# Five norms of a one-layer encoder step: two exact matmuls against a constant matrix and Newton's steps on VectorE, in place of sums by rows, a power on GpSimd and a spread by the identity

## The chip, the core and the metric

The kernel runs on one core of one Trainium2 chip. The metric is device time in microseconds (us) for one launch; less is better. The core's engines are named here as in the profile: TensorE (PE, with its weight loads as PEld), VectorE (DVE), ScalarE (ACT), GpSimd (POOL) and SyncE (SP, which issues most DMAs).

## The reference, cut to what matters

One layer over 320 rows (256 of a prompt, 64 of a running stream), model width 2048, in fp32:

```python
def rmsnorm(x, g):
    y = xf * lax.rsqrt(jnp.mean(xf * xf, axis=-1, keepdims=True) + EPS)
    return y * g
z = rmsnorm(x, ln_g) @ w_in                       # 2048 x 3328: q, k, v, gMLP u and v
q, k = rmsnorm(q, q_g), rmsnorm(k, k_g)           # per head of 64
a_o = sink_attention(...)                         # banded, T5 bias, sinks
s_o = u * (W_s rmsnorm(v) + b)                    # after GELU
mix = concat([rmsnorm(a_o, g_a), rmsnorm(s_o, g_s)])
x = x + mix @ w_out                               # 2048 x 2048
h = rmsnorm(x, ln_ffn)
return x + square(relu(h @ w_up)) @ w_down        # 2048 x 8192, 8192 x 2048
```

The outputs are the new x and the new k, v and normalised v rows.

## The kernel before, in words

Activations are kept transposed: a tile has 128 channels on the partitions and the T = 320 rows of the sequence along the free axis. A norm over channels is therefore a sum over partitions, and its result, one number for each of the 320 rows of the sequence, is needed on every partition.

Every matrix product runs in exact parts: weights and activations are split into a high part (fp32r, a Copy on ScalarE, `w_hi`) and a low part (the difference, on VectorE, `w_lo`), and three matmuls of 128x320 are summed (high x high, low activations x high weights, high activations x low weights), L106 to L138. A weight chunk is 4 tiles of the inner dimension by 256 columns, that is 24 matmuls. `w_hi` and `w_lo` have 3 buffers each, so that the split of a chunk starts when the chunk three places ahead has been used up.

A product of 256 output columns ("a group") is summed in one of two PSUM tiles named `acc` (`ps_acc`, 2 buffers). So group n+2 can't start on TensorE before the result of group n was read out of PSUM. For the product with `w_out` (L464 to L475) a group has 48 matmuls for each half of the inner dimension (half 0: attention, `AH`/`AL`; half 1: gMLP, `SH`/`SL`), and it is read out by

```python
469  nc.vector.tensor_tensor(out=t, in0=ps[:, :, 0:T], in1=rm[:, None, :].to_broadcast([P, 2, T]), op=ALU.mult)
```

The factor `rm`, the inverse root of the mean square of `a_o` or `s_o`, is applied here, after the product, so that the product itself needn't wait for it. The read-out must: it is the first place that needs `rm`. In the same way `rx` (norm of x) is needed by the read-outs of the first product (L257, L258, L267), `rk` (norm of k) by L289, and `r2` by L488.

An inverse root is computed in two functions before. `rstd_rows` (L154) sums squares over partitions by three fp32 matmuls with the data as weights and a column of 1/n as the moving side, so that a row of the sequence lands on a partition; VectorE adds eps, GpSimd takes the power -0.5. `spread` (L165) multiplies these 128x3 numbers, broadcast, with the identity in three fp32 matmuls and copies the 128x320 result out of PSUM. The norm of k does the same for two heads (L261, L283 to L289). An fp32 matmul runs as two passes in the trace. The norm of the gMLP's v (`rv`, L414) uses `rstd_rows` alone.

The order of instructions on each engine is fixed when the program is built: the tile framework schedules by its own timeline, and each engine then works through its list in order. A late instruction thus holds up all that stands behind it in its engine's list.

Of the kernel before, what the change touches and what calls it, by code (L numbers as in the profile page):

```python
# [29 lines left out]
def hymba_step_kernel(ctx: ExitStack, tc: tile.TileContext, i, o):  # L30
    nc = tc.nc

    const = ctx.enter_context(tc.tile_pool(name="const", bufs=1))
    actp = ctx.enter_context(tc.tile_pool(name="actp", bufs=2))
    wp = ctx.enter_context(tc.tile_pool(name="wp", bufs=3))
    sm = ctx.enter_context(tc.tile_pool(name="sm", bufs=2))
    phase1 = ExitStack()
    at = phase1.enter_context(tc.tile_pool(name="at", bufs=2))
# [20 lines left out]
    g_q, g_k = cols[:, 48:49], cols[:, 49:50]  # L59
# [15 lines left out]
    warm_ps = misc()  # L75
    for _ in range(3):
        nc.tensor.matmul(out=warm_ps[:, 0:256], lhsT=idle[:, 0:128], rhs=idle[:, 0:256], start=True, stop=True)
    inv_dm = const.tile([P, 1], F32, name="inv_dm")
    nc.vector.memset(inv_dm, 1.0 / DM)
    inv_1k = const.tile([P, 1], F32, name="inv_1k")  # L80
    nc.vector.memset(inv_1k, 1.0 / 1024)
    hone = const.tile([P, 2], F32, name="hone")
    nc.vector.memset(hone, 0.0)
    nc.vector.memset(hone[0:HD, 0:1], 1.0)
    nc.vector.memset(hone[HD:P, 1:2], 1.0)
    hsel = const.tile([P, 2], F32, name="hsel")
    nc.vector.memset(hsel, 0.0)
    nc.vector.memset(hsel[0:HD, 0:1], 1.0 / HD)
    nc.vector.memset(hsel[HD:P, 1:2], 1.0 / HD)
# [16 lines left out]
    def products(w, k0, nk, jobs, rh, rl, first=None, deep=None):  # L106
# [4 lines left out]
        for a, n in chunks(nk, first is not None):  # L111
# [4 lines left out]
            for j, (c0, ps) in enumerate(jobs):  # L116
# [21 lines left out]
                steps.append((high.ins, low.ins, mm.ins))  # L138

    def sums(name):  # L140

        t = sm.tile([P, TP], F32, name=name, tag="ssq", bufs=2)
        nc.gpsimd.memset(t[:, T:TP], 0.0)
        return t

    def acc_tile():
        return ps_acc.tile([P, 2, 512], F32, name="acc", tag="acc")
# [3 lines left out]
        products(w, k0, nk, [(c0, ps)], rh, rl, deep=deep)  # L151
        return ps

    def rstd_rows(sq, weight, eps, h=1):  # L154

        st = misc()
        for t in range(3):
            nc.tensor.matmul(out=st[:, t * h:t * h + h], lhsT=sq[:, t * P:(t + 1) * P], rhs=weight, start=True, stop=True)  # L158
        r = sm.tile([P, 3 * h], F32, name="r_rows", tag="r_rows")
        nc.vector.tensor_scalar(out=r, in0=st[:, 0:3 * h], scalar1=eps, scalar2=None, op0=ALU.add)  # L160
        rs = sm.tile([P, 3 * h], F32, name="rs_rows", tag="rs_rows")
        nc.gpsimd.tensor_tensor(out=rs, in0=r, in1=nhalf[:, 0:3 * h], op=ALU.pow)
        return rs

    def spread(rs, name):  # L165

        bc = misc()
        for t, (t0, n) in enumerate(TT):
            nc.tensor.matmul(out=bc[:, t0:t0 + n], lhsT=rs[:, t:t + 1].to_broadcast([P, P]),  # L169
                             rhs=ident[:, 0:n], start=True, stop=True)  # L170
        out = sm.tile([P, T], F32, name=name, tag="rstd_b", bufs=2)
        nc.vector.tensor_copy(out=out, in_=bc[:, 0:T])
        return out
# [21 lines left out]
    q0_ps = ps_sc.tile([P, 2, 512], F32, name="q0_ps", tag="s_ps")  # L195
    products(w_in, 0, KT, [(1024, kv_ps), (0, q0_ps)], xh, xl, first=load_x)

    kvx = blk("kvx", [P, 1152])
    kn = kvx[:, 0:448]
    vT = kvx[:, 448:768]  # L200
    rkx = kvx[:, 768:1152].rearrange("p (t c) -> p t c", t=3)
    nc.sync.dma_start(out=kn[:, 256:384], in_=i["ckT"])


# [38 lines left out]
    ssq2 = sm.tile([P, 2, T], F32, name="ssq2", tag="w2", bufs=4)  # L243
    for k in range(0, KT, 2):
        sq = sm.tile([P, 2, T], F32, name="sq2", tag="w2", bufs=4) if k else ssq2
# [2 lines left out]
        if k:  # L248
            nc.vector.tensor_tensor(out=ssq2, in0=ssq2, in1=sq, op=ALU.add)
    ssq = sums("ssq")  # L250
    nc.vector.tensor_tensor(out=ssq[:, 0:T], in0=ssq2[:, 0], in1=ssq2[:, 1], op=ALU.add)

    rx = spread(rstd_rows(ssq, inv_dm, EPS), "rx")


    zk = sm.tile([P, T], F32, name="zk", tag="w2", bufs=4)
    nc.vector.tensor_tensor(out=zk, in0=kv_ps[:, 0, 0:T], in1=rx, op=ALU.mult)  # L257
    nc.vector.tensor_tensor(out=vT, in0=kv_ps[:, 1, 0:T], in1=rx, op=ALU.mult)  # L258
    sq = sums("ksq")
    nc.scalar.activation(out=sq[:, 0:T], in_=zk, func=AF.Square)  # L260
    rk = rstd_rows(sq, hsel, EPS, 2)  # L261

    rq = at.tile([P, 4, 10], F32, name="rq", bufs=1)

    def queries(g, q_ps):
# [8 lines left out]
        for b in range(5):  # L274
# [8 lines left out]
    nc.scalar.activation(out=rkx.rearrange("p t (h d) -> p (t h) d", h=2), in_=rk[:, :, None].to_broadcast([P, 6, HD]),  # L283
                         func=AF.Copy)
    bc = misc()
    for t, (t0, n) in enumerate(TT):
        nc.tensor.matmul(out=bc[:, t0:t0 + n], lhsT=rkx[:, t], rhs=ident[:, 0:n], start=True, stop=True)
    for dst, c in ((kn[:, 0:256], slice(0, 256)), (kn[:, 384:448], slice(256, 320))):
        nc.vector.scalar_tensor_tensor(out=dst, in0=zk[:, c], scalar=g_k, in1=bc[:, c], op0=ALU.mult, op1=ALU.mult)  # L289
    for h in range(2):  # L290
        hs = slice(h * HD, (h + 1) * HD)
        nc.vector.tensor_scalar(out=kz[hs, h, h], in0=kn[hs], scalar1=g_q[hs], scalar2=None, op0=ALU.mult)
# [110 lines left out]
        nc.vector.scalar_tensor_tensor(out=out, in0=c, scalar=1.0, in1=z, op0=ALU.add, op1=ALU.mult)  # L403

    gv = blk("gv", [P, 8, T])
    acc_v = sums("acc_v")
    for g in range(4):
        attend_next((4, 3, 3, 0)[g])
        v_ps = product(w_in, 0, KT, 2304 + g * 256, xh, xl)
# [8 lines left out]
    for t, (t0, n) in enumerate(TT):  # L418
        for h in range(2):
# [3 lines left out]
            dst = vnat[:, t] if t < 2 else vnat_s[0:HD]  # L423
            nc.scalar.activation(out=dst[:, h * 512:(h + 1) * 512], in_=vps[0:n], func=AF.Copy, scale=rv[0:n, t:t + 1])
    nc.gpsimd.dma_start(out=o["sgu_v"], in_=vnat_s[0:HD])
    for g in range(8):
        sp_ps = misc()
        cs = slice(g * P, (g + 1) * P)
        for b in range(2):
# [3 lines left out]
                                in0=sp_ps[:, 0:256].rearrange("p (b i) -> p b i", b=2),  # L433
                                in1=sgb[:, g, None, :].to_broadcast([P, 2, P]), op=ALU.add)
# [136 lines left out]
```

## Time and profile before

| what | value |
|---|---|
| median of 3 runs | 1263.6 us (1261.91 to 1265.82) |
| profiled execution, its own time | 1262.26 us |
| its span | 1259.7 us |
| TensorE busy | 1252.3 us, 99% |
| VectorE busy | 637.9 us, 51% |
| ScalarE busy | 489.4 us, 39% |
| GpSimd busy | 106.1 us, 8% |

The profile is of one execution. A row of its timeline says when an instruction started, how long it took, its engine, its line in the kernel, what it wrote and read, and in square brackets for how long the engine had been idle and what released it. The chain is the sequence of work that ended last, followed back from the end. The profiled execution lies 1.3 us under the median of the runs.

### The profile page before, as it was taken

To read this page: it belongs to the slowest core of one execution; us is meant where nothing else is said; L and a number is where in the kernel's file an instruction comes from. 1 tells how busy PE (TensorE), PEld (TensorE's weight loads), DVE (VectorE), ACT (ScalarE), POOL (GpSimd) and SP (SyncE) were. 2 spreads that over 40 slices of the span, in tenths; PEclk is the share of its full clock that TensorE was granted. 3 is DMA by queue.
4 is the path that set the end of the run, shared out by engine and by line. 5 is a ranking of instruction groups with operands and counts; after the bars stand their busy time and mean duration, and the time that the engine had idled before them with its cause. 6 is when DMAs were issued, how large, how long until landed. Compare 5 with 4: busy or idle time off the path is not lost.

```text
span 1259.7 us, 20182 instructions
## 1 busy us (share of the span) xinstructions
PE 1252.3 (99%) x8519; PEld 1236.6 (98%) x8519; DVE 637.9 (51%) x731; ACT 489.4 (39%) x636; POOL 106.1 (8%) x104
## 2 busy tenths in 40 slices
PE   8999999999999999999999999999999999999998
PEld 7998889999999999999999999999999999999998
DVE  7547857756864444444444444444444334444443
ACT  7335546533543342223333333343333333343221
POOL 2213452400310000000000000000000000000000
PEclk9999999999999999999999999999999999999999
DMA  8643233644454444445544444455444444444550
GB/s 281 191 136 116 85 109 119 216 148 137 151 149 148 152 149 149 149 147 150 150 150 151 150 151 151 151 151 151 150 151 150 146 148 149 148 153 160 169 169 32
DMA packets 186426, 187.77 MB, mean 149 GB/s; under 512 B 6464, under 2 KB 185856, under 8 KB 186336
## 3 DMA queue, kind: packets, MB, share of 16 engines
q1 hardware_dynamic: 185696, 185.43, 47.2%
q8 instruction: 66, 1.08, 0.4%
q0 software_dynamic: 496, 1.03, 0.3%
q14 instruction: 24, 0.20, 0.0%
q10 hardware_dynamic: 144, 0.03, 0.0%
HBM read 182.91 MB, written 3.32 MB: 148 GB/s over the span
## 4 chain that ended last, share of the span: by engine, by line
PE 98%; DMA 0%; SPq 0%; ACT 0%; issue 0%; DVE 0%
PE acc L136 93%; PE misc L136 1%; PE q_ps L136 1%; PE s_ps L329 1%; PE misc L374 1%; PE misc L365 1%; DMA xT<-in_xT 0%; SPq L99 0%; PE misc L275 0%; PE misc L430 0%; PE misc L158 0%; PE misc L422 0%; PE misc L169 0%; ACT XH L178 0%; PE misc L431 0%; ACT w_hi L125 0%
## 5 line engine op out<-in xcount | busy, mean ns | idle before, releaser
L126 DVE TENSOR_TENSOR w_lo<-w_raw,w_hi 128x1024 fp32r<-128x1024 f32 x332 | 413.6, 1246 | 460.6 <-ACT w_hi L125 451.2
L125 ACT ACTIVATE w_hi<-w_raw 128x1024 fp32r<-128x1024 f32 x332 | 351.9, 1060 | 708.0 <-PE acc L136 674.6
L136 PE MATMUL acc<-H2H,w_hi 128*128 128x320 f32 x1024 | 316.6, 309 | 0.0
L136 PE MATMUL acc<-H2L,w_hi 128*128 128x320 f32 x1024 | 316.4, 309 | 0.0
L136 PE MATMUL acc<-H2H,w_lo 128*128 128x320 f32 x1024 | 316.4, 309 | 0.0
L136 PE MATMUL acc<-FH,w_hi 128*128 128x320 f32 x992 | 306.5, 309 | 0.0
L136 PE MATMUL acc<-FL,w_hi 128*128 128x320 f32 x992 | 306.5, 309 | 0.0
L136 PE MATMUL acc<-FH,w_lo 128*128 128x320 f32 x992 | 306.5, 309 | 0.0
L136 PEld LDWEIGHTS acc<-H2L,w_hi 128*128 128x128 f32 x1024 | 192.2, 188 | 0.0
L136 PEld LDWEIGHTS acc<-H2H,w_hi 128*128 128x128 f32 x1024 | 192.2, 188 | 0.0
L136 PEld LDWEIGHTS acc<-H2H,w_lo 128*128 128x128 f32 x1024 | 192.2, 188 | 0.0
L136 PEld LDWEIGHTS acc<-FH,w_hi 128*128 128x128 f32 x992 | 186.2, 188 | 0.0
L136 PEld LDWEIGHTS acc<-FL,w_hi 128*128 128x128 f32 x992 | 186.2, 188 | 0.0
L136 PEld LDWEIGHTS acc<-FH,w_lo 128*128 128x128 f32 x992 | 186.2, 188 | 0.0
L136 PE MATMUL acc<-XH,w_hi 128*128 128x320 f32 x384 | 117.2, 316 | 1.2 <-ACT w_hi L125 1.1
L136 PE MATMUL acc<-XH,w_lo 128*128 128x320 f32 x384 | 116.8, 315 | 0.0
L136 PE MATMUL acc<-XL,w_hi 128*128 128x320 f32 x384 | 116.6, 314 | 0.0
L136 PEld LDWEIGHTS acc<-XH,w_hi 128*128 128x128 f32 x384 | 71.2, 189 | 4.7 <-ACT w_hi L125 2.2
L136 PEld LDWEIGHTS acc<-XL,w_hi 128*128 128x128 f32 x384 | 71.4, 189 | 2.4 <-issue 1.9
L136 PEld LDWEIGHTS acc<-XH,w_lo 128*128 128x128 f32 x384 | 71.1, 188 | 2.2 <-issue 1.5
L488 DVE SCALAR_TENSOR_TENSOR tf<-acc,r 128x640 f32<-128x640 f32 x32 | 26.4, 825 | 42.7 <-PE acc L136 42.7
L502 DVE TENSOR_TENSOR xT<-xT,acc 128x640 f32<-128x640 f32 x31 | 25.5, 821 | 41.8 <-PE acc L136 41.8
(176 smaller groups left out, 1016.9 us busy)
## 6 DMA issues: line engine op xcount, KB each, us to landing
w_raw<-in_w_up SPq DMA_DIRECT2D x128, 512.0 KB
w_raw<-in_w_down SPq DMA_DIRECT2D x128, 512.0 KB
w_raw<-in_w_in SPq DMA_DIRECT2D x44, 512.0 KB
w_raw<-in_w_out SPq DMA_DIRECT2D x32, 512.0 KB
w_first<-in_w_in SPq DMA_DIRECT2D x6, 512.0 KB
out_yT<-xT SPq DMA_DIRECT2D x7, 320.0 KB
xT<-in_xT SPq DMA_DIRECT2D x3, 640.0 KB
w_first<-in_w_in SPq DMA_DIRECT2D x8, 128.0 KB
```

What stands on the lines that cost most here:

```text
L125: high = pin(nc.scalar.activation(out=hi[:, :n], in_=raw[:, :n], func=AF.Copy))
L126: low = pin(nc.vector.tensor_tensor(out=lo[:, :n], in0=raw[:, :n], in1=hi[:, :n].bitcast(F32), op=ALU.subtract))
L136: mm = nc.tensor.matmul(out=out, lhsT=w_[:, k, g * P:(g + 1) * P], rhs=r_(kk), start=(kk == 0 and x == 0), stop=(kk == nk - 1 and x == 2))
L329: nc.tensor.matmul(out=s_ps[:, j, 0:2 * nk].rearrange("x (p k) -> x p k", p=2), lhsT=qT[:, blk_, a:a + 2].rearrange("p a t -> p (a t)"), r ...
L365: nc.tensor.transpose(out=pt_ps[0:n, (2 * p + j) * P:(2 * p + j + 1) * P], in_=s[:, p, j, c:c + n], identity=ident)
L374: nc.tensor.matmul(out=o_ps[p * HD:(p + 1) * HD, 0:256], lhsT=v[0:n, kv], rhs=pt[0:n, p * 256:(p + 1) * 256], start=(x == 0), stop=(x == l ...
L488: nc.vector.scalar_tensor_tensor(out=t, in0=ps[:, :, 0:T], scalar=0.0, in1=r2[:, None, :].to_broadcast([P, 2, T]), op0=ALU.max, op1=ALU.mult)
L502: nc.vector.tensor_tensor(out=xT[:, a:a + n], in0=xT[:, a:a + n], in1=p, op=ALU.add)
```

## The change

Five norms (`rx`, `rk`, `rm0`, `rm1`, `r2`) get a new function `rstd`. The squares, already summed over the tiles of channels, are split into a high part (ScalarE) and a low part (VectorE); two fp32r matmuls of 128x320 with a constant 128x128 matrix as weights (1/2048, 1/1024, or two blocks of 1/64 for the heads of k) give the mean on all partitions at once. Then VectorE works on 128x320 numbers: eps is added, a first guess of the inverse root is made from the integer bits, and three Newton steps of three instructions each follow, that is eleven instructions after the split. The sums lose their padding to 384 columns (only that of v keeps it), and GpSimd writes three constant matrices at the start. `rv` and the norm of q stay as they were.

```diff
@@ constants
-    inv_dm = const.tile([P, 1], F32, name="inv_dm")
-    nc.vector.memset(inv_dm, 1.0 / DM)
+    mean_dm = const.tile([P, P], F32R, name="mean_dm")
+    nc.gpsimd.memset(mean_dm.bitcast(F32), 1.0 / DM)
+    mean_1k = const.tile([P, P], F32R, name="mean_1k")
+    nc.gpsimd.memset(mean_1k.bitcast(F32), 1.0 / 1024)
...
@@ the norm
-        nc.gpsimd.tensor_tensor(out=rs, in0=r, in1=nhalf[:, 0:3 * h], op=ALU.pow)
-    def spread(rs, name):
-        bc = misc()
-        for t, (t0, n) in enumerate(TT):
-            nc.tensor.matmul(out=bc[:, t0:t0 + n], lhsT=rs[:, t:t + 1].to_broadcast([P, P]),
-                             rhs=ident[:, 0:n], start=True, stop=True)
-        out = sm.tile([P, T], F32, name=name, tag="rstd_b", bufs=2)
-        nc.vector.tensor_copy(out=out, in_=bc[:, 0:T])
+    def rstd(acc, mean, eps, out):
+        hl = sm.tile([P, 2, T], F32R, name="n_hl", tag="w2", bufs=4)
+        hi, lo = hl[:, 0], hl[:, 1]
+        nc.scalar.activation(out=hi, in_=acc, func=AF.Copy)
+        nc.vector.tensor_tensor(out=lo, in0=acc, in1=hi.bitcast(F32), op=ALU.subtract)
+        ps = misc()
+        nc.tensor.matmul(out=ps[:, 0:T], lhsT=mean, rhs=hi, start=True, stop=False)
+        nc.tensor.matmul(out=ps[:, 0:T], lhsT=mean, rhs=lo, start=False, stop=True)
+        xt = sm.tile([P, 2, T], F32, name="n_xt", tag="w2", bufs=4)
+        x, t = xt[:, 0], xt[:, 1]
+        nc.vector.tensor_scalar(out=x, in0=ps[:, 0:T], scalar1=eps, scalar2=3e38, op0=ALU.add, op1=ALU.min)
+        nc.vector.tensor_scalar(out=out.bitcast(I32), in0=x.bitcast(I32), scalar1=-0.5, scalar2=float(0x5F3759DF),
+                                op0=ALU.mult, op1=ALU.add)
+        for _ in range(3):
+            nc.vector.tensor_tensor(out=t, in0=out, in1=out, op=ALU.mult)
+            nc.vector.scalar_tensor_tensor(out=t, in0=t, scalar=-0.5, in1=x, op0=ALU.mult, op1=ALU.mult)
+            nc.vector.scalar_tensor_tensor(out=out, in0=t, scalar=1.5, in1=out, op0=ALU.add, op1=ALU.mult)
         return out
...
@@ the five places
-    rx = spread(rstd_rows(ssq, inv_dm, EPS), "rx")
+    rx = rstd(ssq, mean_dm, EPS, rstd_b("rx"))
...
-    rk = rstd_rows(sq, hsel, EPS, 2)
+    rk = rstd(sq, mean_hd, EPS, rstd_b("rk"))
...
-        rm = spread(rstd_rows(acc, inv_1k, EPS), f"rm{half}")
+        rm = rstd(acc, mean_1k, EPS, rstd_b(f"rm{half}"))
...
-    r2 = spread(rstd_rows(acc_x, inv_dm, EPS), "r2")
+    r2 = rstd(acc_x, mean_dm, EPS, rstd_b("r2"))
```

The schedule is built anew, and so the lists of the engines change beyond the five places. On VectorE, at the first norm of the product with `w_out` (`rm` of half 0), the list was, from the split of one weight chunk to that of the next but one (`to` is the read-out of a group, `SL` a low part of the gMLP's output, `xT` the residual add):

```order
L126 TENSOR_TENSOR w_lo<-w_raw,w_hi 128x1024
L172 COPY rm_2640<-misc 128x320
L179 SCALAR_TENSOR_TENSOR SL<-gv,cols,SH 128x320 x2
L469 TENSOR_TENSOR to<-acc,rm_2640 128x640
L471 TENSOR_TENSOR xT<-xT,to 128x640
L126 TENSOR_TENSOR w_lo<-w_raw,w_hi 128x1024
L469 TENSOR_TENSOR to<-acc,rm_2640 128x640
```

One copy stood between the matmul that spread the root and the read-out, and the read-outs of the first and the second group stood one chunk apart.

The same place of VectorE's list now, behind the two `SL` and the first two instructions of the norm (eps, first guess); lines are those of the changed file, `n_xt` holds x and t of the Newton steps:

```order
L182 TENSOR_TENSOR n_xt<-rm_2636 128x320
L130 TENSOR_TENSOR w_lo<-w_raw,w_hi 128x1024
L183 SCALAR_TENSOR_TENSOR n_xt<-n_xt 128x320
L184 SCALAR_TENSOR_TENSOR rm_2636<-n_xt,rm_2636 128x320
L182 TENSOR_TENSOR n_xt<-rm_2636 128x320
L183 SCALAR_TENSOR_TENSOR n_xt<-n_xt 128x320
L130 TENSOR_TENSOR w_lo<-w_raw,w_hi 128x1024
L184 SCALAR_TENSOR_TENSOR rm_2636<-n_xt,rm_2636 128x320
L182 TENSOR_TENSOR n_xt<-rm_2636 128x320
L183 SCALAR_TENSOR_TENSOR n_xt<-n_xt 128x320
L184 SCALAR_TENSOR_TENSOR rm_2636<-n_xt,rm_2636 128x320
L479 TENSOR_TENSOR to<-acc,rm_2636 128x640 x2
```

The read-out of the first group now stands behind all eleven instructions and behind two more weight splits, which are those of the sixth and the seventh chunk of this half; the read-outs of the first two groups stand side by side.

The second norm of this product (half 1) on VectorE now, behind eps, first guess and two instructions of the first step:

```order
L130 TENSOR_TENSOR w_lo<-w_raw,w_hi 128x1024
L184 SCALAR_TENSOR_TENSOR rm_3167<-n_xt,rm_3167 128x320
L182 TENSOR_TENSOR n_xt<-rm_3167 128x320
L183 SCALAR_TENSOR_TENSOR n_xt<-n_xt 128x320
L184 SCALAR_TENSOR_TENSOR rm_3167<-n_xt,rm_3167 128x320
L130 TENSOR_TENSOR w_lo<-w_raw,w_hi 128x1024
L182 TENSOR_TENSOR n_xt<-rm_3167 128x320
L183 SCALAR_TENSOR_TENSOR n_xt<-n_xt 128x320
L184 SCALAR_TENSOR_TENSOR rm_3167<-n_xt,rm_3167 128x320
L479 TENSOR_TENSOR to<-acc,rm_3167 128x640 x2
```

Here the two splits between are those of the fifth and the sixth chunk of the half. Before, one copy (L172) and nothing else stood between a weight split and the read-out.

On TensorE the two matmuls with the constant matrix stand between main matmuls: in half 0 behind 61 and behind 68 of them (the first two groups have 96), in half 1 behind 29 and behind 43, at `rx` behind 6 and behind 9 of the 96 of its group.

## Rows read from the trace of the kernel before

**Rows 1.** The page: busy time of the engines, and the chain by engine.
```profile
PE 1252.3 (99%) x8519; PEld 1236.6 (98%) x8519; DVE 637.9 (51%) x731; ACT 489.4 (39%) x636; POOL 106.1 (8%) x104
...
PE 98%; DMA 0%; SPq 0%; ACT 0%; issue 0%; DVE 0%
```

**Rows 2.** Timeline of TensorE at `r2`: start us, us, engine, line, operation.
```profile
361.69 0.72 PE L158 MATMUL misc<-inv_dm,acc_x 128*128 128x1 f32 x6
...
362.51 0.31 PE L136 MATMUL acc<-H2L,w_hi 128*128 128x320 f32 x1
...
367.20 0.78 PE L169 MATMUL misc<-ident,rs_rows 128*128 128x128 f32 x6
...
368.02 0.31 PE L136 MATMUL acc<-H2L,w_hi 128*128 128x320 f32 x1
```

**Rows 3.** The chain from 367 us on: start us, us, what.
```profile
367.98 874.34 PE acc L136 x5961
```

**Rows 4.** Timeline of TensorE: first matmul of half 0, last of its second group.
```profile
238.45 0.31 PE L136 MATMUL acc<-AH,w_hi 128*128 128x320 f32 x1
...
253.72 0.31 PE L136 MATMUL acc<-AH,w_lo 128*128 128x320 f32 x1
```

**Rows 5.** Timeline of VectorE at the norm of half 0.
```profile
247.35 1.23 DVE L126 TENSOR_TENSOR w_lo<-w_raw,w_hi 128x1024 fp32r<-128x1024 f32 x1 [0.74 <-ACT w_hi L125]
248.50 0.48 DVE L172 COPY rm<-misc 128x320 f32<-128x320 f32 x1
248.90 1.86 DVE L179 SCALAR_TENSOR_TENSOR SL<-gv,cols,SH 128x320 fp32r<-128x320 f32 x2
250.68 0.81 DVE L469 TENSOR_TENSOR to<-acc,rm 128x640 f32<-128x640 f32 x1
251.52 0.82 DVE L471 TENSOR_TENSOR xT<-xT,to 128x640 f32<-128x640 f32 x1
```

**Rows 6.** Timelines of ScalarE and GpSimd in the same stretch.
```profile
248.40 0.55 ACT L178 ACTIVATE SH<-gv,cols 128x320 fp32r<-128x320 f32 x1
250.45 1.06 ACT L125 ACTIVATE w_hi<-w_raw 128x1024 fp32r<-128x1024 f32 x1 [1.50 <-issue]
253.97 1.06 ACT L125 ACTIVATE w_hi<-w_raw 128x1024 fp32r<-128x1024 f32 x1 [2.46 <-PE acc L136]
...
247.76 2.65 POOL L386 TENSOR_TENSOR acc_s<-acc_s,sq 128x320 f32<-128x320 f32 x2 [4.01 <-ACT sq L385]
```

**Rows 7.** Timeline of VectorE: a product out of PSUM, and a tensor_scalar.
```profile
45.05 0.49 DVE L257 TENSOR_TENSOR zk<-acc,rx 128x320 f32<-128x320 f32 x1
...
240.74 0.52 DVE L400 TENSOR_SCALAR gc<-gc 128x640 f32<-128x640 f32 x1
```

**Rows 8.** Timeline of VectorE at the norm of half 1.
```profile
302.59 0.48 DVE L172 COPY rm<-misc 128x320 f32<-128x320 f32 x1
304.69 0.82 DVE L469 TENSOR_TENSOR to<-acc,rm 128x640 f32<-128x640 f32 x1 [1.62 <-PE acc L136]
```

**Rows 9.** Timeline of TensorE: first matmul of the group behind `rx`.
```profile
37.76 0.31 PE L136 MATMUL acc<-XH,w_hi 128*128 128x320 f32 x1
```

**Rows 10.** Timeline of TensorE in the first 14 us.
```profile
1.29 2.93 PE L77 MATMUL misc<-idle 128*128 128x256 f32 x6 [1.29 <-DVE hsel L87]
4.27 0.90 PE L136 MATMUL acc<-XH,w_hi 128*128 128x320 f32 x2
4.97 0.74 PE L136 MATMUL acc<-XL,w_hi 128*128 128x320 f32 x2
...
6.82 0.46 PE L136 MATMUL acc<-XH,w_lo 128*128 128x320 f32 x2
7.12 0.46 PE L136 MATMUL q_ps<-XH,w_lo 128*128 128x320 f32 x2
...
13.51 0.56 PE L136 MATMUL q_ps<-XH,w_hi 128*128 128x320 f32 x2 [1.53 <-ACT w_hi L125]
```

**Rows 11.** Stretches: PE, PEld, DVE, ACT, POOL busy, PEclk, DMA share, GB/s.
```profile
4.00:6.00 2.00, 1.89 (x6) 1.27 (x6) 1.08 (x3) 0.90 (x3) 1.82 (x4) 1.00 0.94 285
```

More of the change, by code (lines that the diff above doesn't have):

```diff
@@ L10 @@
 F32R = mybir.dt.float32r
+I32 = mybir.dt.int32
 AF = mybir.ActivationFunctionType
@@ L77, in hymba_step_kernel @@
         nc.tensor.matmul(out=warm_ps[:, 0:256], lhsT=idle[:, 0:128], rhs=idle[:, 0:256], start=True, stop=True)
-    inv_dm = const.tile([P, 1], F32, name="inv_dm")
-    nc.vector.memset(inv_dm, 1.0 / DM)
     inv_1k = const.tile([P, 1], F32, name="inv_1k")
     nc.vector.memset(inv_1k, 1.0 / 1024)
+    mean_dm = const.tile([P, P], F32R, name="mean_dm")
+    nc.gpsimd.memset(mean_dm.bitcast(F32), 1.0 / DM)
+    mean_1k = const.tile([P, P], F32R, name="mean_1k")
+    nc.gpsimd.memset(mean_1k.bitcast(F32), 1.0 / 1024)
+    mean_hd = const.tile([P, P], F32R, name="mean_hd")
+    nc.gpsimd.memset(mean_hd.bitcast(F32), 0.0)
+    for h in range(2):
+        nc.gpsimd.memset(mean_hd[h * HD:(h + 1) * HD, h * HD:(h + 1) * HD].bitcast(F32), 1.0 / HD)
     hone = const.tile([P, 2], F32, name="hone")
@@ L85, in hymba_step_kernel @@
     nc.vector.memset(hone[HD:P, 1:2], 1.0)
[L86 to L89, printed above, removed]
     loads, between, steps = [], [], []
@@ L140, in sums @@
     def sums(name):
-        t = sm.tile([P, TP], F32, name=name, tag="ssq", bufs=2)
-        nc.gpsimd.memset(t[:, T:TP], 0.0)
-        return t
+        return sm.tile([P, T], F32, name=name, tag="ssq", bufs=2)
     def acc_tile():
@@ L152, in product, with rstd_rows @@
         return ps
-    def rstd_rows(sq, weight, eps, h=1):
+    def rstd_rows(sq, weight, eps):
         st = misc()
         for t in range(3):
[L158 to L161, printed above, removed]
-        nc.gpsimd.tensor_tensor(out=rs, in0=r, in1=nhalf[:, 0:3 * h], op=ALU.pow)
-        return rs
@@ L165, in spread @@
-    def spread(rs, name):
-        bc = misc()
-        for t, (t0, n) in enumerate(TT):
-            nc.tensor.matmul(out=bc[:, t0:t0 + n], lhsT=rs[:, t:t + 1].to_broadcast([P, P]),
-                             rhs=ident[:, 0:n], start=True, stop=True)
-        out = sm.tile([P, T], F32, name=name, tag="rstd_b", bufs=2)
-        nc.vector.tensor_copy(out=out, in_=bc[:, 0:T])
-        return out
+            nc.tensor.matmul(out=st[:, t:t + 1], lhsT=sq[:, t * P:(t + 1) * P], rhs=weight, start=True, stop=True)
@@ new lines, in rstd_rows @@
+        r = sm.tile([P, 3], F32, name="r_rows", tag="r_rows")
+        nc.vector.tensor_scalar(out=r, in0=st[:, 0:3], scalar1=eps, scalar2=None, op0=ALU.add)
+        rs = sm.tile([P, 3], F32, name="rs_rows", tag="rs_rows")
+        nc.gpsimd.tensor_tensor(out=rs, in0=r, in1=nhalf[:, 0:3], op=ALU.pow)
+        return rs
+    def rstd(acc, mean, eps, out):
[15 more added lines that the diff above has]
+            nc.vector.scalar_tensor_tensor(out=out, in0=t, scalar=1.5, in1=out, op0=ALU.add, op1=ALU.mult)
+        return out
@@ L175, in split, with rstd_b @@
+    def rstd_b(name):
+        return sm.tile([P, T], F32, name=name, tag="rstd_b", bufs=2)
     def split(src, g, hi, lo, pinned=False):
@@ L196, in hymba_step_kernel @@
     products(w_in, 0, KT, [(1024, kv_ps), (0, q0_ps)], xh, xl, first=load_x)
-    kvx = blk("kvx", [P, 1152])
+    kvx = blk("kvx", [P, 768])
     kn = kvx[:, 0:448]
     vT = kvx[:, 448:768]
-    rkx = kvx[:, 768:1152].rearrange("p (t c) -> p t c", t=3)
     nc.sync.dma_start(out=kn[:, 256:384], in_=i["ckT"])
@@ L250, in hymba_step_kernel @@
     ssq = sums("ssq")
-    nc.vector.tensor_tensor(out=ssq[:, 0:T], in0=ssq2[:, 0], in1=ssq2[:, 1], op=ALU.add)
-    rx = spread(rstd_rows(ssq, inv_dm, EPS), "rx")
+    nc.vector.tensor_tensor(out=ssq, in0=ssq2[:, 0], in1=ssq2[:, 1], op=ALU.add)
+    rx = rstd(ssq, mean_dm, EPS, rstd_b("rx"))
     zk = sm.tile([P, T], F32, name="zk", tag="w2", bufs=4)
@@ L259, in hymba_step_kernel @@
     sq = sums("ksq")
-    nc.scalar.activation(out=sq[:, 0:T], in_=zk, func=AF.Square)
-    rk = rstd_rows(sq, hsel, EPS, 2)
+    nc.scalar.activation(out=sq, in_=zk, func=AF.Square)
+    rk = rstd(sq, mean_hd, EPS, rstd_b("rk"))
     rq = at.tile([P, 4, 10], F32, name="rq", bufs=1)
@@ L281, in hymba_step_kernel @@
     queries(0, q0_ps)
[L283 to L287, printed above, removed]
     for dst, c in ((kn[:, 0:256], slice(0, 256)), (kn[:, 384:448], slice(256, 320))):
-        nc.vector.scalar_tensor_tensor(out=dst, in0=zk[:, c], scalar=g_k, in1=bc[:, c], op0=ALU.mult, op1=ALU.mult)
+        nc.vector.scalar_tensor_tensor(out=dst, in0=zk[:, c], scalar=g_k, in1=rk[:, c], op0=ALU.mult, op1=ALU.mult)
     for h in range(2):
@@ L405, in hymba_step_kernel @@
     gv = blk("gv", [P, 8, T])
-    acc_v = sums("acc_v")
+    acc_v = at.tile([P, TP], F32, name="acc_v", bufs=1)
+    nc.gpsimd.memset(acc_v[:, T:TP], 0.0)
     for g in range(4):
```

## The prediction

> **What bounds the kernel now.** I read the page's busy times first, then the chain, then the timelines of the engines at each of the five norms. The page shows TensorE busy for 99% of the span, and the chain that ended last is TensorE's work for 98% of it [rows 1]. From 367 us to the end the chain is one unbroken piece of 5961 main matmuls in 874.34 us, 0.1467 us each [rows 3]. The view of waits shows no wait of TensorE from 36 us on that is worth naming. Two things follow. A pass taken off TensorE shortens the run by that pass. And a wait put on TensorE lengthens it by the whole wait, because nothing behind it has slack to give back. The other engines have time to spare on average (VectorE 51%), but each works its list in order, so what counts is when the one instruction that TensorE waits for comes up.
>
> **Passes removed.** At `r2` the six passes that sum by rows start at 361.69, and the second main matmul behind them at 362.51: 0.82 us for six passes and one main matmul, so 0.82 - 0.147 = 0.67 us. The six that spread the root run from 367.20 to 368.02, the same 0.67 [rows 2]. So 1.35 us a norm; the norm of k has the same six and six passes, with two columns in place of one, and I take the same. Five norms: 6.73 us.
>
> **Matmuls added.** Two fp32r matmuls of 128x320 a norm. They are of the main matmuls' shape and kind, so 2 x 0.1467 = 0.29 [rows 3], 1.47 us for five. Net on TensorE: -5.27 us.
>
> **VectorE's chain.** Each norm now has eleven instructions in a row, each needing the one before. A product of 128x320 out of PSUM takes 0.49 us [rows 7], and a dependent instruction starts 0.03 behind the end of the one before (250.68 + 0.81, then 251.52) [rows 5]: 0.52 a step. The first guess is a tensor_scalar out of SBUF; one of 128x640 took 0.52 [rows 7], so half of that with some fixed part, 0.35. Nothing in the trace does integer bits; bounds are 0.25 and 0.52. Together 0.53 + 0.35 + 9 x 0.52 = 5.6 us, without the weight splits that stand between (1.15 us each, from 247.35 to the next start at 248.50 [rows 5]). Before, it was one copy of 0.48. Who waits for it differs at each place.
>
> **`rm` of half 0: a wait of about 5.6 us.** I count on the clock of before from the first matmul of the half, at 238.45 [rows 4]. The second mean matmul stands behind 68 main ones and the first mean: 238.45 + 68 x 0.1467 + 0.15 = 248.57, done 0.31 later at 248.9. VectorE's list has the two `SL` ahead of the norm. The second `SH` that they need ended at 248.95, and beside GpSimd's sums (247.76 to 250.4 [rows 6]) the pair took 1.86 [rows 5]; a little earlier than before, as the copy ahead is gone, they end near 249.8 (bounds 249.4 and 250.6). Then eps, guess and one product: 251.2. Then the split of the sixth chunk, 252.35. Then four steps, 2.1 us: 254.4. Then the split of the seventh chunk. Its `w_hi` can't start before the fourth chunk is used up, which is the last of the second group: 238.45 + 96 x 0.1467 + 0.29 = 252.83. In before `w_hi` started at 253.97, 0.1 behind that point (253.72 is the last matmul, 253.87 its successor [rows 4, 6]), and took 1.06; so it is there at 254.0 and the split runs to 255.55. Four more steps: 257.65. Read-out 0.82: 258.45. TensorE, with the third group next, needs the bank at 252.83. Wait: 5.6 us. Before, the read-out ended at 251.5 [rows 5] against a need at 253.87, a reserve of 2.4 us. The lower bound is firm if steps take what I say: the seventh chunk's split cannot start before 254.05, whatever VectorE did earlier, and 254.05 + 1.15 + 2.1 + 0.82 = 258.1, a wait of 5.3. The upper, with the late end of `SL` and steps of 0.6: 6.8.
>
> **`rm` of half 1: about 1.3 us.** From the first matmul of the half as zero: second mean done at 44 x 0.1467 + 0.31 = 6.8. Eps, guess, two products: 8.7. The fifth chunk's `w_hi` is there at 7.33 + 0.1 + 1.06 = 8.5, so its split ends at 9.85; four steps, 11.95; the sixth chunk's `w_hi` is there at 10.86 + 1.16 = 12.0, split to 13.2; three steps, 14.8; read-out 15.6. TensorE needs the bank at 96 x 0.1467 + 0.29 = 14.4. Wait 1.3, bounds 0.6 and 2.3. Before, the read-out started when the group ended, with `rm` there 1.6 us earlier [rows 8].
>
> **The other three: nothing.** At `rx` the second mean is done at 37.76 + 9 x 0.1467 + 0.15 + 0.31 = 39.5 [rows 9]; eleven steps and two or three splits end near 48.3, and the read-outs of k and v near 49.3. Their bank is needed when the next group but one starts, 96 matmuls behind 37.76, at 52.1: a reserve of 2.8. The next weight split then ends near 51.2 for a need at 52.4, a reserve of 1.2, the smallest of the hidden ones. `rk` feeds k for the attention, which starts some 20 us later. At `r2` a group has 96 matmuls, so 14 us more lie between the mean and the need, and the chain with splits takes some 10. The power on GpSimd, the padding memsets and VectorE's copies go from places where TensorE didn't wait. GpSimd's new constants are written in the first microseconds, while TensorE runs out of data anyway (1.53 us before 13.51 [rows 10]); if that cover were gone, it would be under 1 us. No DMA is added or moved past another; the loads on SP keep their order.
>
> **The clock.** The first main matmuls ran 0.35 us apart (4.27 to 4.97 is two), those at 6.82 and 7.12 0.15 apart [rows 10]: the lower level, 1.2 GHz, and then the upper, 2.4, though the stretch row gives a granted clock of 1.00 there too [rows 11], so I go by the spacing. The lower level held from the first matmul at 1.29 to about 6.5, 5.2 us. After a pause of 1.53 us the level was still the upper one. A pause of 5.6 us does not occur in this trace. If the clock falls in it, I price it by the start: 5.2 us at half pace lose 2.6 us. Bounds 0 and 3.5.
> The Trainium skill, "TensorE: Matmul & The Clock Gate", section "HAM oscillation", says that a long enough wait of TensorE puts the clock back to half and that the matmuls behind the wait start slow. By that rule the clock falls here; the trace's shorter pauses neither show nor exclude it.
>
> **Sum.** -5.27 + 5.6 + 1.3 = +1.6 without the clock, +4.2 with it. Against the profiled execution's 1262.26 us (span 1259.7) that is 1263.9 and 1266.5. The runs' median is 1.3 us higher; on its scale 1265.2 and 1267.8.
>
> **Rivals.**
> (a) *Both waits and the clock falls*: 1267.8. Chance 0.45; my forecast.
> (b) *Both waits, clock stays up*: 1265.2, within 0.3%, not slower. The place is the third group of half 0; it decides whether a pause of 5.6 us is long enough, and all I have is that 1.53 is not. Chance 0.29.
> (c) *No wait at half 0*: TensorE only loses passes, and the time is 1263.6 - 5.3 + 1.3 = 1259.6, or 1258.3 if half 1 doesn't wait either. For that the root must be ready at 252.0, 3.1 us behind the mean, where eleven instructions need 5.6 by the nearest rows; against it speaks also the seventh chunk's split, which alone comes later. It would take VectorE steps at a third of the price, or a third group that doesn't need this read-out. Chance 0.11.
> (d) *The steps are dearer and a third wait appears*: at 0.70 a step, `rx` ends 1.7 us later, which uses up the reserve of 1.2 by 0.5, half 0 waits 0.7 more, half 1 some 1.0 more: 1270. Chance 0.15. The new order of the attention and gMLP stages, whose lists changed too, falls under this.
>
> **How the numbers follow.** A measurement of this kernel can tell about 0.3%, 3.8 us. (a) lies just above that with an own range of 1265.5 to 1269.5, and about 0.65 of it is slower by more than 0.3%; of (b) hardly any, of (d) most: slower 0.29 + 0.02 + 0.14 = 0.45. Faster by over 0.3% is the part of (c) with no wait at all, and something for a stage that I misread: 0.10. The rest, 0.45, within 0.3%. The range of 1260 to 1271 leaves out the better half of (c) and the far end of (d).
>
> **What would show it.** In the profile after: TensorE idle once for 5 to 6 us before the third group of half 0, near 251 us on its clock (the passes saved by then make it some 2 us earlier), released by VectorE's L479; once for about 1.3 us near 308; no wait at the other norms. Main matmuls 0.29 us apart for some microseconds behind the first wait would show (a), 0.147 at once (b). The work of five norms on TensorE falls from 60 passes to 10. Wrong would be: no wait at half 0 (then the steps are cheap), or a wait at `rx`.

## The result and the profile after

The changed kernel took 1269.65 us (median of 4 runs, 1269.37 to 1270.42) against 1264.26 for the kernel before, measured beside it (1261.91 to 1265.82): a ratio of 1.0043, 95% interval 1.0031 to 1.0055. It is slower, by 5.4 us; predicted were +4.2 and 1267.8 us. The profiled execution of after took 1270.42 us, with a span of 1268.6. Executions of one kernel differ by up to some 3 us at the start. Counted from a fixed mark behind the start (the matmul with the one-hot table, which stands at the same place of the program in every run; below it is called the mark), after's trace is 6.0 us longer than either trace of before; the table under "before_again" has this for every run.

The page of after, busy times and the chain, as in [rows 1]:

```profile
PE 1253.2 (99%) x8469; PEld 1237.1 (98%) x8469; DVE 661.2 (52%) x778; ACT 490.4 (39%) x640; POOL 100.8 (8%) x99
...
PE 97%; DVE 1%; DMA 1%; SPq 0%; ACT 0%; issue 0%
```

TensorE has 50 passes fewer (60 gone, 10 added) and yet is busy for longer: some of its work ran slower, in the first 22 us too. VectorE has 47 instructions more, and now holds 1% of the chain, where it had nothing.

TensorE's timeline in after at half 0 of the `w_out` product, from the half's first matmul to the third group:

```profile
240.78 0.31 PE L140 MATMUL acc<-AH,w_hi 128*128 128x320 f32 x1
...
249.73 0.31 PE L174 MATMUL misc<-n_hl,mean_1k 128*128 128x320 f32 x1
...
250.90 0.31 PE L175 MATMUL misc<-n_hl,mean_1k 128*128 128x320 f32 x1
251.04 0.31 PE L140 MATMUL acc<-AH,w_lo 128*128 128x320 f32 x1
...
255.00 0.31 PE L140 MATMUL acc<-AH,w_lo 128*128 128x320 f32 x1
260.95 0.60 PE L140 MATMUL acc<-AH,w_hi 128*128 128x320 f32 x1 [5.63 <-DVE to L479]
261.35 0.47 PE L140 MATMUL acc<-AL,w_hi 128*128 128x320 f32 x1
...
266.42 0.33 PE L140 MATMUL acc<-AH,w_lo 128*128 128x320 f32 x1
266.58 0.31 PE L140 MATMUL acc<-AH,w_hi 128*128 128x320 f32 x1
```

Before, the second group [rows 4] ran into the third without a pause. Now TensorE stands for 5.63 us, and L479 on VectorE, the read-out, ends the wait. Then the matmuls stand 0.267 us apart (19 of them from 261.35 to 266.42) instead of 0.147. Each mean matmul costs just one slot of 0.147. The 5.63 us count from the modelled end of the matmul before, 0.31 us behind its start; as matmuls start every 0.147 us, the slots lost are 260.95 - 255.15 = 5.80 us.

VectorE's timeline in after at the same place, which answers to [rows 5]:

```profile
250.16 2.26 DVE L194 SCALAR_TENSOR_TENSOR SL<-gv,cols,SH 128x320 fp32r<-128x320 f32 x2
252.34 0.48 DVE L178 TENSOR_SCALAR n_xt<-misc 128x320 f32<-128x320 f32 x1
252.85 0.33 DVE L179 TENSOR_SCALAR rm<-n_xt 128x320 int32<-128x320 int32 x1
253.22 0.49 DVE L182 TENSOR_TENSOR n_xt<-rm 128x320 f32<-128x320 f32 x1
253.62 1.22 DVE L130 TENSOR_TENSOR w_lo<-w_raw,w_hi 128x1024 fp32r<-128x1024 f32 x1
254.76 0.49 DVE L183 SCALAR_TENSOR_TENSOR n_xt<-n_xt 128x320 f32<-128x320 f32 x1
255.28 0.49 DVE L184 SCALAR_TENSOR_TENSOR rm<-n_xt,rm 128x320 f32<-128x320 f32 x1
...
256.74 1.22 DVE L130 TENSOR_TENSOR w_lo<-w_raw,w_hi 128x1024 fp32r<-128x1024 f32 x1
...
259.45 0.49 DVE L184 SCALAR_TENSOR_TENSOR rm<-n_xt,rm 128x320 f32<-128x320 f32 x1
259.97 1.55 DVE L479 TENSOR_TENSOR to<-acc,rm 128x640 f32<-128x640 f32 x2
```

From eps at 252.34 to the read-out VectorE never pauses. Where one step needs the last, starts are 0.52 apart (254.76, 255.28); the first guess on integers takes 0.33 and costs 0.37 with its gap.

At half 1 the wait is there too, and shorter (TensorE's timeline in after, third group of half 1):

```profile
321.43 0.39 PE L140 MATMUL acc<-SH,w_hi 128*128 128x320 f32 x1 [1.15 <-DVE to L479]
321.65 0.31 PE L140 MATMUL acc<-SL,w_hi 128*128 128x320 f32 x1
```

In slots that is 1.31 us.

Two stretches of after, columns as in [rows 11], behind the wait of half 0 and behind that of half 1:

```profile
262.00:264.00 2.00, 2.00 (x9) 2.00 (x8) 1.00 (x2) 0.00 (x0) 0.00 (x0) 0.50 0.00 0
322.00:324.00 2.00, 2.00 (x16) 2.00 (x15) 2.00 (x4) 0.09 (x1) 0.00 (x0) 1.00 0.00 0
```

PEclk is 0.50, 1.2 GHz, behind the long wait and stays 1.00 behind the short one; in stretches of equal length the row counts 9 matmuls there and 16 here.

One thing was not in the prediction's sum. TensorE in after near 76 us:

```profile
76.31 2.29 PE L289 MATMUL misc<-hone,qsq 128*128 128x2 f32 x20
78.46 0.41 PE L140 MATMUL acc<-XH,w_hi 128*128 128x320 f32 x1
78.69 0.44 PE L140 MATMUL acc<-XL,w_hi 128*128 128x320 f32 x1
78.93 0.47 PE L140 MATMUL acc<-XH,w_lo 128*128 128x320 f32 x1
79.20 0.47 PE L140 MATMUL acc<-XH,w_hi 128*128 128x320 f32 x1
...
82.13 0.31 PE L140 MATMUL acc<-XH,w_lo 128*128 128x320 f32 x1
```

`hone` is the two-column matrix of the norm of q, which the change doesn't touch. But the schedule was built anew, and the passes of two such norms, ten each, now stand side by side. Behind these twenty, TensorE's matmuls stand 0.267 us apart for 12 starts, without any pause: 12 x 0.12 = 1.4 us. Two pairs of traces below, each with and without this fall of the clock, give 1.5.

A warning on comparing the two profiles: their spans differ by 8.9 us, the medians by 5.4. Of the 8.9 us, 2.9 lie at the start, ahead of 26 us; the run "before_again" below is on that.

### The profile page after: what moved, and what is told of

It reads as the page before. It is cut to its first block, busy times and chain, and to the rows that moved or that the text cites. A ratio compares the mean times of both kernels' runs of the same rounds, so it can differ in the third digit from the quotient of the medians.

```text
span 1268.6 us, 20120 instructions
## 1 busy us (share of the span) xinstructions
PE 1253.2 (99%) x8469; PEld 1237.1 (98%) x8469; DVE 661.2 (52%) x778; ACT 490.4 (39%) x640; POOL 100.8 (8%) x99
## 4 chain that ended last, share of the span: by engine, by line
PE 97%; DVE 1%; DMA 1%; SPq 0%; ACT 0%; issue 0%
PE acc L140 92%; PE misc L140 1%; PE q_ps L140 1%; PE s_ps L338 1%; PE misc L383 1%; DMA xT<-in_xT 1%; PE misc L374 1%; SPq L103 0%; PE misc L289 0%; DVE w_lo L130 0%; PE misc L440 0%; PE misc L432 0%; ACT w_hi L129 0%; DVE SL L194 0%; DVE rm L184 0%
```

## The experiments

The theory, formed from after's trace: the passes save 5.3; VectorE's chain makes TensorE wait for the read-out at both halves, 5.63 + 1.15; the clock falls behind the first wait, 2.5 us (19 x 0.12 and 0.2 at the first matmul); and the twenty thin passes cost 1.4. Sum +5.4. The rivals: the time went at the front (A), or a wait taken away at one place comes back at another (B). Ratios are to the kernel before, run beside each.

**third_tile.** The third group no longer needs the first group's read-out, since the first is summed in the attention's score tile of PSUM, free by then:

```diff
-            ps = product(i["w_out"], 8 * half, 8, g * 256, ...)
+            ps = ps_sc.tile([P, 2, 512], F32, name="s_ps", tag="s_ps") if g == 0 else acc_tile()
+            products(i["w_out"], 8 * half, 8, [(g * 256, ps)], ...)
```

> Changed kernel with one edit: the first group of each half of the w_out product is summed in the score tile of PSUM, which is free by then, so that three groups can stand unread while the norm is worked out; the norm itself is the same. Theory (waits and clock): TensorE no longer waits for the read-out at either half and its clock stays at full level there; the 5.6 and 1.1 us of waits and some 2.7 us of half-level matmuls go, 1269.6 - 9.4 = 1260 us, and the wait rows to L479 are gone from the trace. Rival A (the time went at the front: later xT, the twenty thin norm passes in a row): the waits at w_out go, but less than 4 us come back, 1266 or more. Rival B (another wait takes the place, the weight splits being late behind the chain on VectorE): the third group runs, but a wait of 2 us or more for w_lo appears within 20 us, 1264 or more.

Measured: 1261.07 us, ratio 0.9964 (0.9952 to 0.9977). One wait is left, of 0.33 us, at half 0 in front of the fourth group (TensorE's timeline in third_tile):

```profile
262.94 0.39 PE L140 MATMUL acc<-AH,w_hi 128*128 128x320 f32 x1 [0.33 <-DVE to L480]
```

VectorE does the same chain there (eps at 252.60, last step done at 260.19). By the medians 8.6 us came back of the 9.3 that waits and clock account for; behind the mark it is 9.2 of 9.6 (the waits in slots), and the wait that is left, 0.5 in slots, is about the rest. So the chain as such costs nothing here; what cost was that the third group's bank hung on it. Rivals A and B fall: no wait for `w_lo` appears, and more than 4 us came back.

**early.** The same instructions at other places: half 0's norm in the last group of the product before, half 1's inside half 0 (left out of the diff: the squares and splits of the last group before move up by one weight tile, and a tile is allocated sooner):

```diff
+        if g == 3:
+            rm0 = rstd(acc_a, mean_1k, EPS, rstd_b("rm0"))
...
+            if half == 0 and g == 3:
+                rm1 = rstd(acc_s, mean_1k, EPS, rstd_b("rm1"))
```

> Changed kernel with the two norms of the w_out product worked out earlier: that of half 0 inside the last group of the product before it, that of half 1 after three groups of half 0; same instructions, other places. Theory: both waits for L479's read-out go and with them the fall of the clock, 1269.6 - 9.4 = 1260 us, give or take 2. If the chain of half 0 delays the gate arithmetic of the last group on VectorE and so SH and SL, half 0 doesn't feel it, since SH and SL are first read in half 1. Rival A (front): 1266 or more. Rival B (the chain only moves the wait to where it now stands, because it holds the read-out of the last u group or the weight splits): a new wait of 2 us or more between 225 and 250 us.

Measured: 1264.22 us, ratio 0.9991 (0.9982 to 0.9999). The wait at half 1 is gone; at half 0 one of 3.20 us is left (TensorE's timeline in early):

```profile
258.90 0.39 PE L140 MATMUL acc<-AH,w_hi 128*128 128x320 f32 x1 [3.20 <-DVE to L484]
```

VectorE's timeline in early, from eps to the read-out:

```profile
243.90 0.48 DVE L178 TENSOR_SCALAR n_xt<-misc 128x320 f32<-128x320 f32 x1
...
255.40 0.48 DVE L184 SCALAR_TENSOR_TENSOR rm<-n_xt,rm 128x320 f32<-128x320 f32 x1
255.80 2.21 DVE L194 SCALAR_TENSOR_TENSOR SL<-gv,cols,SH 128x320 fp32r<-128x320 f32 x2
257.94 1.54 DVE L484 TENSOR_TENSOR to<-acc,rm 128x640 f32<-128x640 f32 x2
```

The chain began 8 us sooner but, threaded between the gate arithmetic and the weight splits, took 12 us instead of 7.6, and the `SL` pair, which nothing needs before half 1, still stands ahead of the read-out, 2.1 us long; in after it stood ahead of the chain. I had expected no wait at all and 1260 us: a miss. Behind the mark early is 2.9 us longer than third_tile, about its wait. The instructions are the same, so it is VectorE's order that decides here. In this trace the clock stayed at 1.00 behind 3.20 us.

**wout_old.** The two norms of `w_out` as they were before, the other three new.

> Changed kernel with the two norms of the w_out product put back as they were before (products with a column of 1/1024, root on GpSimd, spread by products with the identity); the other three norms stay new. Theory: no wait for the read-out and full clock at both halves, less the saving of passes there, which goes too (2 x (1.35 - 0.29) = 2.1): 1269.6 - 9.4 + 2.1 = 1262.3 us. The front of the trace is as in the changed kernel: twenty thin norm passes in a row near 76 us and half-level matmuls behind them. Rival A (the time went at the front): 1267 or more. Rival B (w_out was no dearer than before, it only waits elsewhere): the sum of TensorE's waits between 240 and 330 us stays over 4 us.

Measured: 1262.91 us, ratio 0.9987 (0.9978 to 0.9996); no wait of TensorE from 36 us on, PEclk 1.00 at both halves, and the clock's fall behind the twenty thin passes as in after. It is 1.8 us dearer than third_tile, which has the new norms there without their waits: the price of the passes, sized 2.1. Behind the mark it is 1.5, and 2.0 with the wait of 0.5 that third_tile still has.

**one_step** and **six_steps.** One or six Newton steps instead of three at `w_out` (`for _ in range(steps_n)`; with one, these two roots are less exact).

> Changed kernel with one Newton step instead of three for the two norms of the w_out product (so those two roots are less exact). Theory: each step is three dependent instructions of 0.52 us, two steps less make the chain 3.1 us shorter: the wait at half 0 falls from 5.6 to 2.5 us, that at half 1 (1.1) to nothing. If the clock falls behind a wait of 2.5 us as it did behind 5.6, the time is 1269.6 - 3.1 - 1.1 = 1265.4; if it stays, 2.7 less, 1262.7. Rival (the wait is set by the weight splits between the steps, not by the steps): the wait at half 0 stays over 4 us.

> Changed kernel with six Newton steps instead of three for the two norms of w_out. Theory: three steps more are nine dependent instructions of 0.52 us, 4.7 us on each chain, and weight splits that come due meanwhile stand between them, 1.1 us each: the wait at half 0 is 5.6 + 4.7 to 5.8, 10.3 to 11.5 us, that at half 1 1.1 + 4.7 to 5.8, 5.8 to 7.0. Behind the wait at half 1, which now is as long as that at half 0 was, the clock falls too (2.7 us more). Time 1269.6 + 4.7 + 4.7 + 2.7 = 1281.7, up to 1284. Rival (half 0's fall of the clock belongs to its place, not to the wait's length): PEclk stays 1.00 behind the wait at half 1, 1279 to 1281.

Measured: 1262.27 us, ratio 0.9978 (0.9969 to 0.9987), for one step; 1279.53 us, ratio 1.0128 (1.0113 to 1.0143), for six. TensorE's timeline in one_step at half 0 (at half 1 there is no wait):

```profile
256.94 0.39 PE L140 MATMUL acc<-AH,w_hi 128*128 128x320 f32 x1 [1.46 <-DVE to L479]
```

And in six_steps, at both halves:

```profile
261.96 0.61 PE L140 MATMUL acc<-AH,w_hi 128*128 128x320 f32 x1 [10.37 <-DVE to L479]
...
328.19 0.60 PE L140 MATMUL acc<-SH,w_hi 128*128 128x320 f32 x1 [7.30 <-DVE to L479]
```

Three steps more: 10.37 - 5.63 = 4.74 us, nine instructions of 0.527. At half 1, 6.15 more: nine steps and one split of 1.15 that came due, 5.9, and 0.3 in which VectorE stood idle ahead of that split (at 321.87), as its `w_hi` wasn't there yet. Two steps less: 4.17 us, which is 3.1 and one split of 1.1 that the shorter chain no longer lets in before the read-out. The forecast of 2.5 us had left that split out, and its rival was right that far: splits between the steps are part of the wait. At half 1 the fall of the clock follows the length of the wait, not the place (stretches of six_steps):

```profile
322.00:324.00 2.00, 0.00 (x0) 0.00 (x0) 1.97 (x3) 0.00 (x0) 0.00 (x0) 1.00 0.21 72
...
328.00:330.00 2.00, 1.81 (x7) 1.85 (x8) 2.00 (x4) 0.46 (x1) 0.00 (x0) 0.50 0.00 0
```

The rival of the place falls by this row, though the time, forecast at 1281.7, came within the rival's 1279 to 1281. Behind the mark six_steps is 11.9 us longer than after: 4.7 and 6.2 of waits, 1.5 for the new fall of the clock at half 1, and 0.4 less for that at half 0, which cost 2.2 here and 2.5 in after. Its profiled execution, at 1278.68 us, also has a shorter start than after's, by 3.7 us, which is part of why the times lie closer together than 11.9. Behind one_step's wait of 1.46 us PEclk is 1.00.

**best.** third_tile, and the thin passes of the third query norm held back:

```diff
+        if g == 3:
+            with tc.issue_after(steps[0][2]):
+                norm(2, sq_2)
```

> Changed kernel with two edits: the third PSUM tile for the first group of each half of w_out, and the ten thin passes (128x2) of the third query norm held back until after the first weight tile of the next product, so that no twenty stand in a row. Theory: as with the third tile alone no wait over 0.5 us at w_out, and the fall of the clock from 79 to 82 us goes too, 1.6 us: 1261.1 - 1.6 = 1259.5 us, PEclk 1.00 in every window from 60 to 100 us. Rival (the clock falls there for another reason, such as the norm of k or the load of the other engines): half level stays near 80 us and the time stays at 1261.

Measured: 1260.1 us, ratio 0.9966 (0.9953 to 0.9979). The passes stand ten at a time (TensorE's timeline in best):

```profile
76.08 1.17 PE L295 MATMUL misc<-hone,qsq 128*128 128x2 f32 x10
```

and the stretch behind them in best has the full clock:

```profile
78.00:80.00 2.00, 2.00 (x16) 2.00 (x15) 0.00 (x0) 0.95 (x1) 1.52 (x1) 1.00 0.78 243
```

It is faster than both kernels. Against third_tile it is 1.0 us in the medians, and the intervals don't tell these two apart; behind the mark it is 1.5, for an expected 1.6. Against before it is 4.7 there, and as best still has a wait of 0.33 (0.5 in slots), the passes themselves save 5.2.

**thin_twice, thin_twice_b, thin_thrice.** The kernel before, with its ten thin passes run two or three times in a row:

```diff
-        for b in range(5):
+        for b in [0, 1, 2, 3, 4] * (2 if g == 2 else 1):
```

> The kernel before with the ten passes (128x2) of the third query norm run twice into the same bank, twenty in a row near 76 us as in the changed kernel; nothing else moves. Theory (a row of twenty thin passes takes the clock down): 10 more passes of 0.115 us are 1.2 us, and main matmuls behind them stand 0.27 us apart for some 3 us, 1.6 us more: 2.8 us over the kernel before, PEclk 0.50 in a window behind 79 us. Rival (the clock fell there for another reason, with the thin passes beside it): the passes cost 1.2 us and PEclk stays 1.00.

> The kernel before with twenty thin passes in a row, a second execution's trace. If the first trace (clock at full level behind them) stands for the kernel, PEclk is 1.00 again from 76 to 90 us; if it was a matter of where the passes fell in time, this one may show 0.50.

> The kernel before with the ten thin passes of the third query norm run three times into the same bank, thirty in a row (3.4 us). With twenty in a row the clock stayed at full level in that kernel. If thin passes count as too little work for the clock when there are enough of them, PEclk is 0.50 in a window behind them and the main matmuls stand 0.27 us apart; if they never do by themselves, PEclk stays 1.00 and the row costs its 2.3 us alone.

Measured: thin_twice 1265.8 us, ratio 1.0013 (1.0004 to 1.0022), its trace without a fall of the clock; thin_twice_b, the same kernel, with one; thin_thrice, one execution, 1268.99 us, with one. A stretch behind the row in thin_twice:

```profile
82.00:84.00 2.00, 2.00 (x16) 2.00 (x15) 0.10 (x1) 0.00 (x0) 1.82 (x1) 1.00 0.79 250
```

The same in thin_twice_b:

```profile
78.00:80.00 2.00, 2.00 (x10) 2.00 (x10) 0.17 (x1) 0.00 (x0) 1.46 (x1) 0.56 0.75 207
```

And in thin_thrice:

```profile
84.00:86.00 2.00, 2.00 (x9) 2.00 (x9) 0.00 (x0) 0.00 (x0) 1.38 (x1) 0.50 0.05 17
```

Twenty thin passes in a row can take the clock down in the kernel before, with nothing else changed, but don't do so in every execution. Behind the mark thin_twice is 1.1 us longer than before, the price of the ten passes alone, and thin_twice_b 2.7: the fall costs 1.5, as between third_tile and best. thin_thrice is 3.8 longer, 2.2 for twenty passes and again 1.5. The medians of thin_twice, +1.6 us, lie between.

**twenty_later.** As best, but the passes of the second and third query norm held back together:

> The version with the third tile, with the thin passes of the second and third query norm (10 + 10, 128x2) held back together until after the first weight tile of the next product: twenty in a row again, but 12 us behind the two transposes of v that stand 3 us ahead of them in the changed kernel. Theory 1 (twenty thin passes in a row of two norms take the clock down by themselves): main matmuls 0.27 us apart for some 3 us behind them, PEclk 0.50 there. Theory 2 (it takes the transposes 3 us ahead as well): PEclk 1.00 in every window from 60 to 100 us.

One execution, 1260.45 us: twenty in a row at 85.77, PEclk 1.00 behind them. That fits theory 2, but after thin_twice_b a single trace without the fall proves little. In all six traces of kernels that kept the changed kernel's order at this place (after, third_tile, early, wout_old, one_step, six_steps) the clock fell. Why always there stays open.

**before_again.** The kernel before, once more:

> The kernel before once more, for a second look at its first 24 us. In the kernel before as profiled TensorE waited 1.5 us at 13.5 us and kept full clock; in the changed kernel and in four kernels made from it it waited 2.8 to 3.2 us and the clock then stood at half level up to 21 us, 1.5 to 3.4 us lost. Theory A (the change brings this, by its new order or constants): wait 1.5 us and full clock again, span near 1259.7. Theory B (the arrival of the fourth xT piece differs from execution to execution, and the first profile of the kernel before was a lucky one): a wait of 2.8 us or more and half level behind it, span near 1262.

Measured: 1264.65 us, span 1262.9. TensorE's first long wait, in the timeline of before_again:

```profile
14.48 0.61 PE L136 MATMUL q_ps<-XH,w_hi 128*128 128x320 f32 x2 [2.73 <-ACT w_hi L125]
16.79 2.50 PE L136 MATMUL acc<-XH,w_hi 128*128 128x320 f32 x8 [0.64 <-ACT w_hi L125]
```

And in that of after:

```profile
14.88 0.56 PE L140 MATMUL q_ps<-XH,w_hi 128*128 128x320 f32 x2 [2.82 <-ACT w_hi L129]
17.19 2.46 PE L140 MATMUL acc<-XH,w_hi 128*128 128x320 f32 x8 [1.13 <-ACT w_hi L129]
```

Theory B, though the wait lies just under the 2.8 that it asked for. The wait of 1.53 us in the first profile of before [rows 10] was a short one; here it is 2.73, and the eight passes behind it take 2.50 us, at half level, as in after. The single matmul with the one-hot table is a fixed mark in the program. TensorE's timelines in before, before_again and after have it at:

```profile
23.05 0.60 PE L228 MATMUL misc<-oneh,tab 32*16 32x255 f32 x2
...
26.22 0.60 PE L228 MATMUL misc<-oneh,tab 32*16 32x255 f32 x2
...
25.96 0.60 PE L242 MATMUL misc<-oneh,tab 32*16 32x255 f32 x2
```

So the late start needs no change of the kernel. Counted from this mark to the start of TensorE's last matmul, the start drops out, and both traces of before give the same time:

| trace | mark, us | last matmul, us | between, us | against before, us |
|---|---|---|---|---|
| before | 23.05 | 1256.08 | 1233.0 | |
| before_again | 26.22 | 1259.25 | 1233.0 | 0.0 |
| after | 25.96 | 1265.00 | 1239.0 | +6.0 |
| third_tile | 26.22 | 1256.09 | 1229.9 | -3.2 |
| early | 26.36 | 1259.09 | 1232.7 | -0.3 |
| wout_old | 26.38 | 1257.77 | 1231.4 | -1.6 |
| one_step | 26.14 | 1257.12 | 1231.0 | -2.0 |
| six_steps | 22.26 | 1273.23 | 1251.0 | +17.9 |
| best | 25.72 | 1254.10 | 1228.4 | -4.7 |
| thin_twice | 26.59 | 1260.73 | 1234.1 | +1.1 |
| thin_twice_b | 22.95 | 1258.63 | 1235.7 | +2.7 |
| thin_thrice | 26.70 | 1263.51 | 1236.8 | +3.8 |
| twenty_later | 26.62 | 1254.92 | 1228.3 | -4.7 |

For after the terms give -5.2 (passes, from best) + 5.80 + 1.31 (the waits in slots) + 2.5 (clock) + 1.5 (thin passes) = 5.9 of the 6.0.

## Why the prediction was right, step by step

| step | predicted, us | measured, us |
|---|---|---|
| passes, net | -5.3 | -5.2 (best against before, behind the mark) |
| wait at half 0 | 5.6 (5.3 to 6.8) | 5.63, in slots 5.80 |
| wait at half 1 | 1.3 (0.6 to 2.3) | 1.15, in slots 1.31 |
| clock behind the first wait | 2.6 (0 to 3.5) | 2.5 |
| `rx`, `rk`, `r2` | 0 | no wait in the trace |
| thin passes side by side | not seen | 1.5 |
| sum | +4.2 | +5.4 by the medians, +6.0 behind the mark |

The mechanism held as written. On the clock of the half (first matmul as zero) the prediction had the third group's bank due at 14.38 and the read-out done at 20.0; the trace has 14.37 (240.78 plus 98 slots) and the start of the third group at 20.17. This worked because the working counted VectorE's list, splits included, instead of its 51% load. The steps were 0.52 as taken, the guess 0.37 for 0.35. The `SL` pair ended 0.2 later than taken. At half 1 the prediction's own terms, 15.6 - 14.4, give 1.2, not 1.3.

The places were forecast at 251 and 308 us; TensorE stops at 255.3 and 320.3. 2.9 us of that are the later start and 1.5 the thin passes. The rest at half 1, some 8 us, is the first wait and the clock behind it, which the forecast of 308 left out though the sum has them.

The clock was the one open choice, at 0.45 against 0.29, and it fell as in (a). At this place two rows now stand around it: 3.20 us without a fall (early), 5.63 with one. The Trainium skill, "TensorE: Matmul & The Clock Gate", section "HAM oscillation", on which the prediction leant for this, is borne out by the 5.63 us here and by the 10.37 and 7.30 of six_steps.

The price of that fall, 2.6 us, was taken from the start, and that 2.5 came out is luck: behind the longer waits of six_steps the fall cost 2.2 and 1.5. The 0.35 us that the prediction read as the spacing of the lower level has gaps of the start in it; at half level the spacing is 0.267.

What was missed is the 1.5 us near 79 us. The prediction put the new order of the attention and gMLP stages under rival (d), whose mechanism is dearer steps and a third wait, not a clock that falls while TensorE never stops. The order of the passes is fixed when the program is built, so the twenty side by side could have been looked for in the list. That GpSimd's new constants cost nothing fits: TensorE's first main matmul starts at 4.28 us in after as in before_again, and the mark at 25.96 lies between the two of before. But the start varies by 3 us by itself, so a cost of well under 1 us isn't excluded.

And rival (c) named the way out that third_tile then took: "a third group that doesn't need this read-out". It forecast 1258.3 without any wait, 5.3 under a median of 1263.6. best came to 1260.1, 4.1 under the kernel before measured beside it (1264.2), and 4.7 behind the mark, where its last wait makes the difference to the 5.2 of the passes.

## What to carry to other kernels

When a chain on a lightly loaded engine replaces something short, write down its list between the input and the instruction that frees the next PSUM bank, splits of other chunks included, and compare the end with the moment at which TensorE needs that bank. If it is late, look for one more bank that TensorE can go on with: that gave back 9.2 us here with the chain as it is (third_tile), more than two Newton steps fewer (one_step, 8.0), which made the roots less exact. And look through a rebuilt schedule for thin passes that came to stand side by side.

## What the runs showed of the hardware

- TensorE's clock fell to half (spacing 0.267 instead of 0.147 us, PEclk 0.50) behind waits of 5.63, 7.30 and 10.37 us; it didn't behind 1.15, 1.46 and 3.20, all in the `w_out` product, one trace each. The falls cost 2.5 us (behind 5.63), 1.5 (7.30) and 2.2 (10.37): not in the order of the waits. At the start, where TensorE still has other gaps beside the wait, it fell around 2.25 (best), 2.73 (before_again) and 2.82 (after), but not around 1.53 (before).
- It can fall without any wait: behind twenty passes of 128x2 in a row, which the page counts as busy, in six traces of six in the changed order, in one of two of the kernel thin_twice, with thirty in the one trace of thin_thrice, and not in twenty_later. It cost 1.5 us each time that a pair of traces can tell. Ten in a row didn't do it in before, before_again and best.
- A dependent VectorE step of 128x320 costs 0.52 us, of which 0.03 is the gap; the guess on integers out of SBUF 0.33, eps out of PSUM 0.48.
